# Matmuls of one weight group in series by width in place of alternation, in a two-layer decoder trunk

## Chip, cores and metric

One Trainium2 chip, one core. The metric is the device time of one execution in microseconds; the median of three runs is taken.

## What is computed

Two pre-norm residual layers on 256 tokens of width 2048, in float32. Each layer has three groups of attention heads over one shared normalised input, an output projection, and a gated MLP of inner width 5632 with a causal convolution over three tokens. Cut to its frame:

```python
for l in range(DEPTH):
    h = _rmsnorm(x, attn_norm[l])
    z = jnp.einsum('bsd,de->bse', h, w_in[l])
    ...
    mix = jnp.concatenate([o_a, o_b, o_c], axis=-1)
    x = x + jnp.einsum('bsm,md->bsd', mix, w_o[l])
    h = _rmsnorm(x, ffn_norm[l])
    x = x + _conv_gated_mlp(h, ffn_w_up[l], ffn_conv_w[l], ffn_conv_b[l], ffn_w_down[l])
return _rmsnorm(x, final_norm)
```

## The kernel before

All activations lie transposed, features on the 128 partitions and the 256 tokens along the free axis. All weights lie in HBM as one stream of 128x128 blocks in the order of their use. `load` brings 16 blocks at a time into a `raw` tile (three buffers). `convert` takes a group of 8 blocks (`SUB`) and splits each weight into a rounded part `hi` (line 134, a cast on ScalarE, ACT in the profile) and the rest `lo` (line 135, a subtraction on VectorE, DVE); `hi` and `lo` have four buffers each. An activation tile is split in the same way: it holds 512 columns, the high parts of the 256 tokens and then their low parts. The product to full accuracy is then weight `hi` times all 512 columns, plus weight `lo` times the first 256; the halves of the 512 result columns are added at the end (`total`, lines 227 and 229, or the additions into `x`, lines 726 and 727).

`mm_t` (lines 175 to 189) does this for one output tile of 128 features. It takes a PSUM bank (three under the name `mm`), goes over the k blocks of the inner width and issues two matmuls for each: the 512-column one with `hi` (line 184) and the 256-column one with `lo` (line 185), in alternation. The last block of a chain has them the other way round (lines 187 and 188), so that the chain ends on the 512-column one. `weights`, called for each block, starts the conversion two groups ahead, and the load of later chunks, at the first block of a group. `hooks` lets a chain form the column of the norm (`inv_rms`, line 324) after half of its blocks.

Chains of `mm_t` are: the input projections (k = 16), the output projection in two passes (k = 10 and k = 6, 16 chains each), the up projection of the MLP (k = 16, 88 chains a layer in two halves of 44) and the down projection (k = 22, 16 chains for each half). The stream is counted in groups of 8 from its start. In layer 0 the blocks after the narrow projections begin in the middle of a group, so an up chain there covers 4, 8 and 4 blocks of three groups; in the MLP of layer 1 it covers two whole groups.

Three other helpers use the same stream and are not touched. `mm_t2` does two output tiles at once at the start of a layer. `mm_v` (lines 208 to 223) makes tiles with tokens on the partitions: the activation is stationary, the weights `hi` and `lo` are the moving operand, three matmuls of 512 or 256 columns for each step (lines 218 to 220). `narrow` issues three matmuls of 256 columns for each block (lines 678 to 680). The Tile framework puts the instructions of each engine in order by priority and dependence, so small steps of other work stand between the chains on TensorE (PE), such as attention (lines 386 to 419).

Of the kernel before, what the change touches and what calls it, by code (L numbers as in the profile page):

```python
# [17 lines left out]
T = 256  # L18
# [10 lines left out]
SUB = 8  # L29
# [29 lines left out]
def kernel(ctx: ExitStack, tc: tile.TileContext, xin, pos, wstream, cst, par, fin, out):  # L59
    nc = tc.nc  # L60
# [14 lines left out]
    def slot(dtype=F32):  # L75
        return slots.tile([P, 2 * T], dtype, tag="slot", name=nm("slot"))
# [10 lines left out]
    def bank(tag, bufs):  # L87
        return psum.tile([P, 512], F32, tag=tag, name=nm(tag), bufs=bufs)
# [8 lines left out]
    bounds = [(i, min(SUB, nblk - i)) for i in range(0, nblk, SUB)]  # L97
    sub_of = {b: s for s, (at, n) in enumerate(bounds) for b in range(at, at + n)}

    def load(c):  # L100
        if c >= nch or c in raws:
            return
        n = min(CH, nblk - c * CH)
        t = wpool.tile([P, CH * P], F32, tag="raw", name=nm("raw"), bufs=3)
        nc.sync.dma_start(
            t[:, : n * P], wflat[c * CH * P * P : (c * CH + n) * P * P].rearrange("(p e) -> p e", p=P)
        )
        raws[c] = t
# [12 lines left out]
    def convert(s, between=None):  # L121
        if s >= len(bounds) or s in subs:
            return
        at, n = bounds[s]
        c = at // CH
        load(c)
        o = (at - c * CH) * P
        src = raws[c][:, o : o + n * P]
        hi = wpool.tile([P, SUB * P], F32R, tag="hi", name=nm("hi"), bufs=4)
        lo = wpool.tile([P, SUB * P], F32R, tag="lo", name=nm("lo"), bufs=4)  # L130
        step = SUB // 2 * P if c < 3 else SUB * P
        for o in range(0, n * P, step):
            a = slice(o, min(o + step, n * P))
            nc.scalar.copy(hi[:, a], src[:, a])  # L134
            nc.vector.tensor_tensor(lo[:, a], src[:, a], f(hi[:, a]), ALU.subtract)  # L135
            if between is not None:
                between()
        subs[s] = (hi, lo)

    def weights(b, n=1):  # L140
        s = sub_of[b]
        at = bounds[s][0]
        if b == at:
            convert(s)
            convert(s + 1)
            convert(s + 2)
            load(b // CH + 1)
            load(b // CH + 2)
        o = (b - at) * P
        hi, lo = subs[s]  # L150
        return hi[:, o : o + n * P], lo[:, o : o + n * P]

    cb = [0]
# [21 lines left out]
    def mm_t(moving, hooks={}, tag="mm", bufs=3):  # L175
        ps = bank(tag, bufs)
        k = len(moving)
        for i, mv in enumerate(moving):
            if i in hooks:
                hooks[i]()  # L180
            hi, lo = weights(cb[0])
            cb[0] += 1
            if i < k - 1:
                nc.tensor.matmul(ps, hi, mv, start=(i == 0), stop=False)  # L184
                nc.tensor.matmul(ps[:, :T], lo, mv[:, :T], start=False, stop=False)  # L185
            else:
                nc.tensor.matmul(ps[:, :T], lo, mv[:, :T], start=(i == 0), stop=False)  # L187
                nc.tensor.matmul(ps, hi, mv, start=False, stop=True)  # L188
        return ps

    def mm_t2(moving, hooks={}):
# [287 lines left out]
    for l in range(DEPTH):  # L479
# [4 lines left out]
        if l == 0:  # L484
            first = mm_t2(hx)
            convert(4)
            convert(5)
            squares()
            first.append(mm_t(hx))
            first.append(mm_t(hx, {KT // 2: norm.cols}, "s", 2))  # L490
        else:
            first = mm_t2(hx, {KT // 2: norm.cols})
# [62 lines left out]
        for j in range(2):  # L555
            for h in range(H_FOX):
                if j == 0:
                    fqk.append(slot())
                i = j * H_FOX + h + 1
                u = total(first[i] if i < len(first) else mm_t(hx))  # L560
                nc.gpsimd.tensor_tensor(fqk[h][:, j * T : (j + 1) * T], u, rstd if j else rstd_f, ALU.mult)
                tick()
# [100 lines left out]
        mv = [slot() for _ in range(3)]  # L663
# [52 lines left out]
        for m in range(KT):  # L716
            ps = mm_t([mix[i] for i in order])
# [6 lines left out]
        for m in range(KT):  # L724
            ps = mm_t([mix[i] for i in range(4, 10)])
# [5 lines left out]
        for half in range(2):  # L731
            acts = []
            for i in range(HALF):
                ft = half * HALF + i
                ys = []
                for j in range(2):
                    ps = mm_t(hx, {KT // 2: norm.cols} if rstd is None else {})
# [23 lines left out]
            for m in range(KT):  # L761
                ps = mm_t(acts)
# [136 lines left out]
```

## Time and profile before

| | |
|---|---|
| median of 3 runs | 2298.94 us (2298.13 to 2301.83) |
| span of the profiled execution | 2297.5 us, 1.4 us under the median |
| PE busy | 2270.6 us, 99% |
| VectorE busy | 1580.0 us, 69% |
| ScalarE busy | 1234.2 us, 54% |
| HBM traffic | 178 GB/s over the span |
| granted TensorE clock | 0.997 of full speed |

All times in the profile are of one execution and count from the start of its span. A row of the timeline has a start and a duration. PE's durations are latencies: matmuls overlap in the array, so the distance between the starts of two rows, and not the duration, says how long one holds the engine. Line numbers are those of the kernel before.

### The profile page before, as it was taken

What the parts mean: (1) busy time and instruction counts of PE and PEld (TensorE: products, weight loads), DVE (VectorE), ACT (ScalarE), POOL (GpSimd) and SP (SyncE); (2) the same over time, 40 slices, a digit from 0 to 9 for tenths busy, and PEclk for the clock granted to TensorE, in tenths of its full rate; (3) what the DMA queues carried; (4) which work ended last, traced back from release to release, by engine and by line L of the source; (5) the groups of instructions that cost most, each with busy time, mean ns of one, the idle gap of its engine ahead of it and who ended that gap; (6) DMA issues with size and microseconds to landing.
All of it is one profiled execution on the core that took longest, in us unless ns stands there. A gap on an engine that the chain in (4) does not pass through costs nothing.

```text
span 2297.5 us, 33344 instructions
## 1 busy us (share of the span) xinstructions
PE 2270.6 (99%) x12956; PEld 1965.8 (86%) x12956; DVE 1580.0 (69%) x2512; ACT 1234.2 (54%) x1878; POOL 447.6 (19%) x445
## 2 busy tenths in 40 slices
PE   8999999999999999999999999999999999999997
PEld 7888988888888888888888889888888888888886
DVE  7768768777765577776664777687777556777654
ACT  6456645655543455554454665466555435555543
POOL 5500002222210022221140110032222001222211
PEclk9999999999999999999999999999999999999999
DMA  7544434555555555555555444345555555555553
GB/s 257 186 163 165 149 140 171 183 183 186 188 187 190 184 184 185 185 191 185 189 185 183 152 162 164 129 173 189 188 184 183 186 187 191 188 184 183 185 186 116
DMA packets 60062, 410.59 MB, mean 179 GB/s; under 512 B 6912, under 2 KB 7040, under 8 KB 11136
## 3 DMA queue, kind: packets, MB, share of 16 engines
q1 hardware_dynamic: 59184, 407.40, 49.8%
q8 instruction: 101, 1.65, 0.3%
q10 hardware_dynamic: 720, 1.07, 0.1%
q14 instruction: 57, 0.47, 0.1%
HBM read 406.35 MB, written 2.10 MB: 178 GB/s over the span
## 4 chain that ended last, share of the span: by engine, by line
PE 96%; DVE 3%; issue 1%; ACT 0%; DMA 0%; POOL 0%; DVEq 0%; ACTq 0%
PE mm L184 52%; PE mm L185 26%; PE mm L188 3%; PE mm L218 2%; PE mm L219 2%; PE mm L220 2%; PE s L386 2%; PE mm L187 2%; DVE h L360 1%; PE mm L205 1%; DVE lo L135 1%; PE mm L678 1%; PE mm L679 1%; PE mm L680 1%; PE pv L418 1%
## 5 line engine op out<-in xcount | busy, mean ns | idle before, releaser
L135 DVE TENSOR_TENSOR lo<-raw,hi 128x1024 fp32r<-128x1024 f32 (+1 forms) x775 | 988.7, 1276 | 454.3 <-ACT hi L134 449.7
L184 PE MATMUL mm<-h,hi 128*128 128x512 f32 x3435 | 1225.4, 399 | 0.6 <-DVE x L727 0.6
L134 ACT CAST hi<-raw 128x1024 fp32r<-128x1024 f32 (+1 forms) x775 | 807.4, 1042 | 596.7 <-PE mm L184 444.8
L185 PE MATMUL mm<-h,lo 128*128 128x256 f32 x3435 | 964.1, 281 | 0.0
L184 PEld LDWEIGHTS mm<-h,hi 128*128 128x128 f32 x3435 | 645.5, 188 | 151.6 <-issue 1.7
L185 PEld LDWEIGHTS mm<-h,lo 128*128 128x128 f32 x3435 | 648.5, 189 | 9.8
L184 PE MATMUL mm<-slot,hi 128*128 128x512 f32 x1792 | 640.0, 399 | 3.4 <-DVE x L727 3.4
L185 PE MATMUL mm<-slot,lo 128*128 128x256 f32 x1792 | 503.1, 281 | 0.0
L184 PEld LDWEIGHTS mm<-slot,hi 128*128 128x128 f32 x1792 | 336.7, 188 | 87.0 <-issue 5.1
L185 PEld LDWEIGHTS mm<-slot,lo 128*128 128x128 f32 x1792 | 338.4, 189 | 4.7
L741 POOL TENSOR_TENSOR tmp<-tmp,rstd 128x256 f32<-128x256 f32 x176 | 131.1, 745 | 736.3 <-DVE tmp L229 721.2
L227 ACT COPY tmp<-mm 128x256 f32<-128x256 f32 (+1 forms) x233 | 86.7, 372 | 161.1 <-PE mm L188 159.5
L749 POOL TENSOR_TENSOR tmp<-tmp,tmp 128x256 f32<-128x256 f32 x88 | 120.2, 1366 | 268.6 <-ACT tmp L748 264.9
L355 POOL TENSOR_TENSOR tmp<-tmp,tmp 128x256 f32<-128x256 f32 x64 | 78.5, 1227 | 454.1 <-ACT tmp L350 453.3
L744 ACT ACTIVATE tmp<-tmp,par 128x256 f32<-128x256 f32 x176 | 105.7, 601 | 66.5 <-POOL tmp L741 66.4
L229 DVE TENSOR_TENSOR tmp<-mm,tmp 128x256 f32<-128x256 f32 (+1 forms) x233 | 97.6, 419 | 53.2 <-ACT tmp L227 53.1
L424 DVE TENSOR_TENSOR slot<-tmp,slot 128x256 fp32r<-128x256 f32 x96 | 41.2, 429 | 92.5 <-ACT slot L423 92.5
L423 ACT CAST slot<-tmp 128x256 fp32r<-128x256 f32 x96 | 39.0, 406 | 108.0 <-POOL tmp L749 106.3
L188 PE MATMUL mm<-h,hi 128*128 128x512 f32 x229 | 91.4, 399 | 0.0
L746 DVE SCALAR_TENSOR_TENSOR tmp<-tmp,par,tmp 128x254 f32<-128x254 f32 x176 | 85.0, 483 | 6.2
L745 DVE SCALAR_TENSOR_TENSOR tmp<-tmp,par,tmp 128x255 f32<-128x255 f32 x176 | 83.3, 473 | 1.3 <-ACT tmp L744 1.3
L218 PE MATMUL mm<-hi,h 128*128 128x512 f32 (+1 forms) x192 | 68.3, 356 | 0.0
(183 smaller groups left out, 1815.0 us busy)
## 6 DMA issues: line engine op xcount, KB each, us to landing
raw<-in_w SPq DMA_DIRECT2D x381, 1024.0 KB, 4.8
raw<-in_w SPq DMA_DIRECT2D x12, 256.0 KB, 5.4
x<-in_x SPq DMA_DIRECT2D x8, 256.0 KB, 5.3
out<-x SPq DMA_DIRECT2D x4, 256.0 KB, 2.3
out<-x ACTq DMA_DIRECT2D x4, 256.0 KB, 2.4
raw<-in_w SPq DMA_DIRECT2D x1, 512.0 KB, 3.4
par<-in_par SPq DMA_DIRECT2D x1, 325.0 KB, 6.3
par<-in_par SPq DMA_DIRECT2D x1, 304.0 KB, 5.2
```

What stands on the lines that cost most here:

```text
L134: nc.scalar.copy(hi[:, a], src[:, a])
L135: nc.vector.tensor_tensor(lo[:, a], src[:, a], f(hi[:, a]), ALU.subtract)
L184: nc.tensor.matmul(ps, hi, mv, start=(i == 0), stop=False)
L185: nc.tensor.matmul(ps[:, :T], lo, mv[:, :T], start=False, stop=False)
L188: nc.tensor.matmul(ps, hi, mv, start=False, stop=True)
L218: nc.tensor.matmul(ps[t][:, :n], s_hi, hi, start=(i == 0), stop=False)
L227: nc.scalar.copy(t[:rows], ps[:rows, T : 2 * T])
L229: nc.vector.tensor_tensor(u[:rows], ps[:rows, :T], t[:rows], ALU.add)
L741: nc.gpsimd.tensor_tensor(uu, u, rstd, ALU.mult)
L744: nc.scalar.activation(y, uu, AF.Identity, scale=q_[:, w + 2 : w + 3], bias=q_[:, w + 3 : w + 4])
L746: nc.vector.scalar_tensor_tensor(y[:, 2:], uu[:, : T - 2], q_[:, w : w + 1], y[:, 2:], ALU.mult, ALU.add)
L749: nc.gpsimd.tensor_tensor(ys[0], ys[0], ys[1], ALU.mult)
```

## The change

`mm_t` cuts its blocks into runs that lie in one group of 8. For each run it asks for all weights first, and then issues all 512-column matmuls of the run as one series and all 256-column ones as another. In the first run of a chain the wide series leads (the first matmul has to write all 512 columns of the bank), in the last the narrow one leads (the chain ends wide), and in runs between the wide one leads. In a chain of one run the last wide matmul stands behind the narrow series. The hooks of a run are called ahead of the whole run.

```diff
--- before.py
+++ after.py
@@ -175,17 +175,27 @@
     def mm_t(moving, hooks={}, tag="mm", bufs=3):
         ps = bank(tag, bufs)
         k = len(moving)
-        for i, mv in enumerate(moving):
-            if i in hooks:
-                hooks[i]()
-            hi, lo = weights(cb[0])
-            cb[0] += 1
-            if i < k - 1:
-                nc.tensor.matmul(ps, hi, mv, start=(i == 0), stop=False)
-                nc.tensor.matmul(ps[:, :T], lo, mv[:, :T], start=False, stop=False)
-            else:
-                nc.tensor.matmul(ps[:, :T], lo, mv[:, :T], start=(i == 0), stop=False)
-                nc.tensor.matmul(ps, hi, mv, start=False, stop=True)
+        runs, i = [], 0
+        while i < k:
+            n = min(k - i, SUB - (cb[0] + i - bounds[sub_of[cb[0] + i]][0]))
+            runs.append(range(i, i + n))
+            i += n
+        for r, run in enumerate(runs):
+            for i in run:
+                if i in hooks:
+                    hooks[i]()
+            ws = [weights(cb[0] + i) for i in run]
+
+            def high(part):
+                for i in part:
+                    nc.tensor.matmul(ps, ws[i - run[0]][0], moving[i], start=(i == 0), stop=(i == k - 1))
+
+            n = len(run) if r < len(runs) - 1 else len(run) - 1 if r == 0 else 0
+            high(run[:n])
+            for i in run:
+                nc.tensor.matmul(ps[:, :T], ws[i - run[0]][1], moving[i][:, :T], start=False, stop=False)
+            high(run[n:])
+        cb[0] += k
         return ps
 
     def mm_t2(moving, hooks={}):
```

In the changed file the wide matmuls have line 191 and the narrow ones line 196; other lines behind `mm_t` are 10 higher.

What the order of PE has at the border of two up chains of layer 0 (banks `mm_9249` and `mm_9307`; `h` are the activation tiles, `hi_9225` and `lo_9226` one weight group), before:

```order
L184 MATMUL mm_9249<-h_3722,hi_9225 128x512
L185 MATMUL mm_9249<-h_3722,lo_9226 128x256
L187 MATMUL mm_9249<-h_3723,lo_9226 128x256
L188 MATMUL mm_9249<-h_3723,hi_9225 128x512
L184 MATMUL mm_9307<-h_3708,hi_9225 128x512
L185 MATMUL mm_9307<-h_3708,lo_9226 128x256
L184 MATMUL mm_9307<-h_3709,hi_9225 128x512
L185 MATMUL mm_9307<-h_3709,lo_9226 128x256
```

And the same place now:

```order
L196 MATMUL mm_9249<-h_3722,lo_9226 128x256
L196 MATMUL mm_9249<-h_3723,lo_9226 128x256
L191 MATMUL mm_9249<-h_3720,hi_9225 128x512
L191 MATMUL mm_9249<-h_3721,hi_9225 128x512
L191 MATMUL mm_9249<-h_3722,hi_9225 128x512
L191 MATMUL mm_9249<-h_3723,hi_9225 128x512
L191 MATMUL mm_9307<-h_3708,hi_9225 128x512
L191 MATMUL mm_9307<-h_3709,hi_9225 128x512
L191 MATMUL mm_9307<-h_3710,hi_9225 128x512
L191 MATMUL mm_9307<-h_3711,hi_9225 128x512
L196 MATMUL mm_9307<-h_3708,lo_9226 128x256
L196 MATMUL mm_9307<-h_3709,lo_9226 128x256
```

The four blocks that end one chain and the four that begin the next are in the same group; their wide matmuls now form one series of eight, with narrow series of four on either side of it (the one ahead is the end of a longer one).

The place of the norm column in the first up chain of layer 0 (line 324 before, 334 now; `tmp_3743` is the sum of squares), before:

```order
L185 MATMUL mm_4103<-h_3718,lo_4055 128x256
L184 MATMUL mm_4103<-h_3719,hi_4054 128x512
L185 MATMUL mm_4103<-h_3719,lo_4055 128x256
L324 MATMUL misc_4124<-cs,tmp_3743 128x1 x2
L184 MATMUL mm_4103<-h_3720,hi_4082 128x512
L185 MATMUL mm_4103<-h_3720,lo_4083 128x256
```

And now:

```order
L196 MATMUL mm_4103<-h_3717,lo_4055 128x256
L196 MATMUL mm_4103<-h_3718,lo_4055 128x256
L334 MATMUL misc_4112<-cs,tmp_3743 128x1 x2
L196 MATMUL mm_4103<-h_3719,lo_4055 128x256
L196 MATMUL mm_4103<-h_3720,lo_4083 128x256
L196 MATMUL mm_4103<-h_3721,lo_4083 128x256
```

The column's matmuls stand at nearly the same place in PE's order, now between two narrow matmuls of the middle run.

## Rows read from the trace of the kernel before

**Rows 1.** The page: busy us of the engines, and the chain that ended last.

```profile
PE 2270.6 (99%) x12956; PEld 1965.8 (86%) x12956; DVE 1580.0 (69%) x2512; ACT 1234.2 (54%) x1878; POOL 447.6 (19%) x445
...
PE 96%; DVE 3%; issue 1%; ACT 0%; DMA 0%; POOL 0%; DVEq 0%; ACTq 0%
```

**Rows 2.** Waits: engine and line, for whom, us in total, times, longest.

```profile
ACT hi L134 <- PE mm L184: 444.8, 350, 3.6
...
PE mm L202 <- DVE h L360: 7.1, 1, 7.1
...
PE s L185 <- DVE lo L135: 0.3, 1, 0.3
```

**Rows 3.** Groups of PE by shape: count | busy us, mean ns | idle before.

```profile
L184 PE MATMUL mm<-h,hi 128*128 128x512 f32 x3435 | 1225.4, 399 | 0.6 <-DVE x L727 0.6
...
L184 PE MATMUL mm<-slot,hi 128*128 128x512 f32 x1792 | 640.0, 399 | 3.4 <-DVE x L727 3.4
...
L188 PE MATMUL mm<-h,hi 128*128 128x512 f32 x229 | 91.4, 399 | 0.0
...
L188 PE MATMUL mm<-slot,hi 128*128 128x512 f32 x128 | 51.3, 400 | 0.1
```

**Rows 4.** Busy time by stretch: one up projection, one `mm_v`, one `narrow`.

```profile
core 0: us, PE busy (x) PEld busy (x) DVE busy (x) ACT busy (x) POOL busy (x), PEclk, DMA share, GB/s
775.59:1018.68 243.09, 243.09 (x1378) 210.80 (x1376) 173.27 (x235) 141.85 (x211) 60.28 (x62) 1.00 0.53 186
88.53:109.61 21.08, 21.08 (x94) 17.46 (x93) 10.42 (x9) 8.76 (x10) 0.87 (x2) 1.00 0.56 199
277.98:287.81 9.83, 9.83 (x84) 9.83 (x83) 8.71 (x21) 6.57 (x11) 0.00 (x0) 1.00 0.42 142
```

**Rows 5.** PE's timeline, up projection: start us, duration us; from first to last, three pairs.

```profile
800.20 0.28 PE L185 MATMUL mm<-h,lo 128*128 128x256 f32 x1
...
801.02 0.40 PE L184 MATMUL mm<-h,hi 128*128 128x512 f32 x1
801.26 0.28 PE L185 MATMUL mm<-h,lo 128*128 128x256 f32 x1
```

**Rows 6.** PE's timeline, first and last row of twelve pairs of a down projection.

```profile
667.48 0.28 PE L185 MATMUL mm<-slot,lo 128*128 128x256 f32 x1
...
671.64 0.28 PE L185 MATMUL mm<-slot,lo 128*128 128x256 f32 x1
```

**Rows 7.** PE's timeline, from `mm_t` into the series of 512 of `mm_v`.

```profile
87.84 0.40 PE L188 MATMUL mm<-h,hi 128*128 128x512 f32 x1
88.07 0.40 PE L218 MATMUL mm<-hi,h 128*128 128x512 f32 x1
88.31 0.39 PE L219 MATMUL mm<-lo,h 128*128 128x512 f32 x1
```

**Rows 8.** PE's timeline, from 512 to 256 inside `mm_v`: first and seventeenth of 256.

```profile
109.84 0.28 PE L218 MATMUL mm<-hi,h 128*128 128x256 f32 x1
...
111.75 0.28 PE L219 MATMUL mm<-lo,h 128*128 128x256 f32 x1
```

**Rows 9.** PE's timeline, `mm_v` after an attention block: the ends of six steps.

```profile
182.87 0.39 PE L219 MATMUL mm<-lo,h 128*128 128x512 f32 x1
...
184.25 0.39 PE L219 MATMUL mm<-lo,h 128*128 128x512 f32 x1
```

**Rows 10.** DVE's timeline, the low part of one group.

```profile
800.77 1.23 DVE L135 TENSOR_TENSOR lo<-raw,hi 128x1024 fp32r<-128x1024 f32 x1 [1.16 <-ACT hi L134]
```

**Rows 11.** PE's timeline, the norm column in layer 0's first up chain.

```profile
405.32 0.61 PE L324 MATMUL misc<-cs,tmp 128*128 128x1 f32 x4 [1.39 <-DVE tmp L355]
```

**Rows 12.** PE's timeline, end of a chain of `mm_t` and start of the next.

```profile
775.11 0.28 PE L185 MATMUL mm<-slot,lo 128*128 128x256 f32 x1
...
775.35 0.40 PE L188 MATMUL mm<-slot,hi 128*128 128x512 f32 x1
...
775.82 0.28 PE L185 MATMUL mm<-h,lo 128*128 128x256 f32 x1
```

## The prediction

> **What bounds the kernel now.** I read the page's busy table first, then the chain that ended last, the waits of TensorE, the groups by shape, and then the timeline and the table by stretches to see what one matmul costs beside its neighbours. TensorE is busy for 2270.6 of 2297.5 us and 96% of the chain is PE [rows 1]. Its waits for other engines are few: the largest is 7.1 us once at the start, and one for a converted `lo` tile, 0.3 us [rows 2]. So the time is the sum of the distances from one matmul's start to the next one's, and a change of order on PE is worth what it does to these distances.
>
> The pairs that the change touches are 3435 + 1792 from lines 184 and 185, 229 + 128 from the ends of their chains [rows 3], and 16 of the one chain in another bank, `s`: 5600 in all. The 399 ns that the groups name for a wide matmul is a latency, and latencies overlap. What counts is the spacing. A long stretch of the up projection gives it: 243.09 us for 43 chains of 16 pairs, so 243.09 / 688 = 353.3 ns a pair, at clock 1.00 (the upper level, 2.4 GHz) and with PE busy throughout [rows 4]. Seen singly, three pairs take 1.06 us, from 800.20 to 801.26, and the last 512-column matmul of them holds the engine for 0.24 us [rows 5].
>
> The same trace has series of one width, in the value and narrow projections, each matmul with a weight load of its own as in the pairs. In `mm_v` 93 steps of 512 columns take 21.08 us, 226.7 ns each; in `narrow` 82 steps of 256 columns take 9.83 us, 119.9 ns each, and the counts of weight loads go with those of matmuls [rows 4]. One of each is 346.6 ns, 6.7 ns less than a pair in alternation. That alternation can also run at that pace is seen at 667.48 to 671.64 us: 12 pairs in 4.16 us, 346.7 ns [rows 6]. The extra 6.7 ns is thus not in the columns; it belongs to how the two widths fall on each other in most chains.
>
> **The change, part by part.** *What it removes.* In the written order of the changed program a 512-column matmul follows a 256-column one 571 times among these pairs, against 5240 before; the rest stand in series, mostly of 8 and 16 with some of 4 where a chain begins in the middle of a group. Of the 5600 pairs 4224 are in the MLP (176 up chains of 16, 64 down chains of 22), nearly all at 353.3: 4224 x 6.7 = 28.3 us. The other 1376 (input and output projections) lie between the two paces, so between 0 and 9.2 us; I take 6, two thirds, as both paces occur there. Together 34 us, if every matmul went at the pace of a series.
>
> *What it adds.* Each border between series has a price. From 256 to 512 it is in the trace once at full length: after a chain's last 256s, the 512s at 87.84, 88.07 and 88.31, and then 226.7 each [rows 4]. The first two take 0.47 us against 0.453, 17 ns too much, and the 0.01 us of the rows allows 10 ns either way [rows 7]. From 512 to 256 the first sixteen take 1.91 us (109.84 to 111.75) against 1.92, so nothing, or a few ns gained [rows 8]. A round trip costs some 13 ns (17 less a few), and 571 of them 7.5 us. From both sides: nothing where series fall together as the alternation at 346.7 does; and 20 ns where a series needs as long to settle as it does after an attention block, six steps in 1.38 us (182.87 to 184.25) against 1.36 [rows 9], which makes 11.4 us. I take 7.5, because rows 7 is the same border, from 256 in `mm_t` to 512.
>
> *What it moves.* No instruction is added on any engine and every chain still ends on a 512-column matmul, so the copies out of the bank begin where they did. Weights are asked for at the same place, the first block of a group. In a group that begins with the low series `lo` is needed one matmul earlier, 0.24 us; a `hi` tile in a leading series comes free about 1 us (8 x 0.12) earlier, a `lo` tile in a leading series up to 1.8 (8 x 0.227), and neither later. What covers this is the lead of the conversions: ACT waits 444.8 us in 350 waits for PE to free a `hi` buffer and PE waited 0.3 us for `lo` in all [rows 2], so conversions are ahead by nearly the whole buffer depth. If the cover were gone, the price would be a DVE conversion of 1.23 us [rows 10] per group, far above the gain; I cost it at nothing. DVE and ACT keep their work, 173 and 142 of 243 us in an up stretch [rows 4], so 1.5% less time there does not make either the bound. The hook that forms the norm column is written four pairs earlier in the first up chain of layer 0, yet its matmuls stay at the same place of PE's order, after seven of the eight narrow matmuls of the middle run; PE waits 1.39 us there now [rows 11] and reaches it a little sooner, at most 0.1 us more wait. The 32 short chains of the second output pass in both layers also wait on additions into x; if these set the pace there, 192 x 6.7 = 1.3 us of the gain is not had, which I take off by 0.5.
>
> *Sum.* 34 - 7.5 - 0.5 = 26 us off the profiled span of 2297.5, so 2271.5. The median of the runs, 2298.94, lies 1.4 us above that span, for what is around it; the same above the new one gives 2272.9, say 2273 us.
>
> A rule speaks against any gain, and is a rival below. The Trainium skill, "TensorE: Matmul & The Clock Gate", section "Back-to-back issue gap", gives the warm spacing as the matmul's own columns over 2.4 GHz plus about 2.5 ns. By it a pair is an estimated 325 ns in whatever order, and the sum would be no change. The trace does not agree: 353.3 and 346.7 ns for the same two widths.
>
> **The rivals.** *Series settle as slowly as after attention.* Then 571 x 20 = 11.4 us are given back in place of 7.5: gain 22, 2277 us. This is inside my range. In the other direction, borders that cost nothing give 34 us, 2265.
>
> *A series of 512 in `mm_t` does not settle (slower).* What the trace has of `mm_t` itself is only two 512s in a row at the ends of chains, and these take 0.47 us for two (775.35 to 775.82), 235 each; the two 256s ahead of them take 0.24, 120 each [rows 12]. At these rates a pair in series costs 355 ns, 1.7 more than now, and 5600 pairs cost 9.5 us: 2308. It decides from 233.3 ns per 512 (353.3 less 120): above, the change loses. For it: these are the very operands (moving `h`, stationary `hi`), while `mm_v` swaps their roles and uses one stationary operand twice. Against it: the two 512s of rows 7 start the same way with 0.23 and 0.24 and the third is at pace, and the weights are loaded for each matmul in both.
>
> *Width alone counts.* The cost of a pair would lie in something other than the order, say in the chains' operands, and it stays at 353: 2299, no change. The 346.7 in rows 6, with the operands of the down projection in alternation, speaks against it, and for it that I cannot say why a chain falls into one pace or the other.
>
> That the change does not do what it says is closed by the order: the series are there.
>
> **How the numbers follow.** About 0.2% (4.6 us) is what a measurement of this kernel can tell from no change. My forecast, with slow or free borders in it, has 0.82: 2263 to 2284, the lower end being the whole 34 us with 2 us of error in the rest, the upper one slow borders and 7 us for waits that I cost at nothing. Width alone 0.07, a series that does not settle 0.08, and 0.03 for waits of the conversions that eat half of the gain, which is still faster or just within 0.2%. So faster 0.85, same 0.07, slower 0.08, and the range leaves out the last three cases.
>
> **What would show it.** In the changed profile an up stretch of layer 1, 43 chains, should take about 43 x (16 x 346.7 + 13) = 239.1 us in place of 243.09, and in layer 0, where chains begin in the middle of a group and have two round trips, 239.6. Within a chain the timeline should show 512s at 0.23, 0.24 and then 226 to 227 ns over the rest, and 256s at 120. PE's waits for `lo` and `hi` should stay under 1 us. It is wrong if 512s in series stay near 235, if a pair is still 353, or if new waits for lines 134 and 135 appear in front of a series.

## The result and the profile after

| | before | after |
|---|---|---|
| median | 2298.53 us, 4 runs (2296.55 to 2301.83) | 2278.24 us, 4 runs (2277.20 to 2278.74) |
| ratio, 95% interval | | 0.9909 [0.9895, 0.9923] |
| span of the profiled execution | 2297.5 us | 2275.4 us |

The changed kernel is 20.3 us faster by the medians and 22.1 us by the spans. The forecast was 26 us less, 2273 us in a range of 2263 to 2284. So the direction and the range hold, and the gain came out 4 us smaller than forecast by the spans and over 5 by the medians. (The profiled execution is the fastest of the four, so the new median lies 2.8 us above the new span and not 1.4 as before.)

The page of the changed kernel, busy us of the engines and the chain that ended last by engine:

```profile
PE 2247.6 (99%) x12956; PEld 1970.5 (87%) x12956; DVE 1574.5 (69%) x2512; ACT 1221.3 (54%) x1878; POOL 424.6 (19%) x445
...
PE 96%; DVE 2%; issue 1%; ACT 1%; DMA 0%; SPq 0%; DVEq 0%; ACTq 0%
```

It has the shape of [rows 1]: PE bounds the kernel at 99%, with 23.0 us less of it. The waits of TensorE, and the largest wait of the conversions for it, in the columns of [rows 2]:

```profile
PE mm L212 <- DVE h L370: 6.6, 1, 6.6
PE misc L334 <- DVE tmp L365: 5.2, 3, 2.0
PE mm L191 <- DVE x L737: 3.9, 8, 1.1
...
PE mm L196 <- ACT slot L433: 0.8, 2, 0.4
PE mm L213 <- DVE lo L135: 0.3, 1, 0.3
...
ACT hi L134 <- PE mm L191: 352.1, 286, 4.0
```

The waits are nearly the old ones; only that for `slot`, 0.8 us, is new. None for line 134 or 135 stands in front of a series, and ACT still waits hundreds of microseconds for PE to free `hi` buffers, so the conversions kept their lead. One wait has grown, that for the norm column (line 334, 324 before): it was 3.4 us in two waits. More of it below. The groups by shape, to be read against [rows 3]:

```profile
L191 PE MATMUL mm<-h,hi 128*128 128x512 f32 x3664 | 908.7, 393 | 0.0
L196 PE MATMUL mm<-h,lo 128*128 128x256 f32 x3664 | 493.9, 282 | 0.0
L191 PE MATMUL mm<-slot,hi 128*128 128x512 f32 x1920 | 486.2, 393 | 3.9 <-DVE x L737 3.9
```

The mean latency of a wide matmul fell from 399 to 393 ns. That is about the gain of a pair, but the spacing is what decides. From here on a *border* is a place where the width changes, and a *round trip* is one change from narrow to wide and one back. Two up halves of 44 chains by stretch, from the first matmul's start to the last one's, in the columns of [rows 4]. The first is in layer 0 (chains over 4, 8 and 4 blocks), the second in layer 1 (chains over two whole groups):

```profile
766.67:1012.25 245.58, 245.58 (x1409) 216.13 (x1408) 173.84 (x241) 144.27 (x216) 61.35 (x64) 1.00 0.53 189
1892.98:2137.69 244.71, 244.71 (x1409) 216.30 (x1407) 175.91 (x239) 140.57 (x216) 47.40 (x64) 1.00 0.53 189
```

The 704 pairs of such a stretch at the series' pace, 226.67 + 120.00 = 346.67 ns by the unrounded starts, less the last wide matmul, which the window leaves out, are 243.83 us. Layer 1 is 0.88 us above that, or **20 ns for each of 44 chains**, which have one round trip each. Layer 0 is 1.75 us above it, 20 ns for each of 88 round trips. Before, the two stretches took 248.5 us each from first start to last start; this is where the time came from. How a series runs is seen on the timeline of PE (start us, duration us). Layer 0 first, and then layer 1, where series of 16 meet across chains:

```profile
572.59 2.00 PE L191 MATMUL mm<-h,hi 128*128 128x512 f32 x8
574.43 1.60 PE L196 MATMUL mm<-h,lo 128*128 128x256 f32 x12
575.86 0.86 PE L191 MATMUL mm<-h,hi 128*128 128x512 f32 x3
```
```profile
1930.11 3.82 PE L191 MATMUL mm<-h,hi 128*128 128x512 f32 x16
1933.76 2.08 PE L196 MATMUL mm<-h,lo 128*128 128x256 f32 x16
1935.67 3.82 PE L191 MATMUL mm<-h,hi 128*128 128x512 f32 x16
```

From start to start eight wide ones take 1.84 us, and 8 x 226.7 is 1.81; sixteen take 3.65 against 3.63. Both have about 0.02 to 0.03 us too much whatever their length, so it is lost at the start of the series. The narrow ones take 1.43 for 12 (1.44 at pace) and 1.91 for 16 (1.92), and give back up to 10 ns at theirs. By the unrounded starts the wide distances after a settled narrow series are 233, 236, 228, 233, 231 and then 227 ns, and the narrow ones begin with 113, 119, 120. Together that is 27 ns too much in the wide series and 8 too little in the narrow one, the 20 ns again.

### The profile page after: what moved, and what is told of

The parts are those of the page before. It is cut to its first block, busy times and chain, and to the rows that moved or that the text cites. A ratio compares the mean times of both kernels' runs of the same rounds, so it can differ in the third digit from the quotient of the medians.

```text
span 2275.4 us, 33362 instructions
## 1 busy us (share of the span) xinstructions
PE 2247.6 (99%) x12956; PEld 1970.5 (87%) x12956; DVE 1574.5 (69%) x2512; ACT 1221.3 (54%) x1878; POOL 424.6 (19%) x445
## 3 DMA queue, kind: packets, MB, share of 16 engines
q10 hardware_dynamic: 720, 1.07, 0.1%
## 4 chain that ended last, share of the span: by engine, by line
PE 96%; DVE 2%; issue 1%; ACT 1%; DMA 0%; SPq 0%; DVEq 0%; ACTq 0%
PE mm L191 55%; PE mm L196 28%; PE mm L228 2%; PE mm L229 2%; PE mm L230 2%; PE s L396 2%; DVE h L370 1%; PE mm L688 1%; PE mm L690 1%; PE mm L689 1%; PE pv L428 1%; DVE lo L135 1%; PE misc L349 0%; PE mm L215 0%; PE misc L334 0%
## 5 line engine op out<-in xcount | busy, mean ns | idle before, releaser
L191 PE MATMUL mm<-h,hi 128*128 128x512 f32 x3664 | 908.7, 393 | 0.0
L191 PEld LDWEIGHTS mm<-h,hi 128*128 128x128 f32 x3664 | 665.6, 189 | 125.4 <-issue 1.7
L196 PEld LDWEIGHTS mm<-h,lo 128*128 128x128 f32 x3664 | 484.9, 191 | 27.3 <-DVE lo L135 0.2
L196 PE MATMUL mm<-h,lo 128*128 128x256 f32 x3664 | 493.9, 282 | 0.0
L191 PE MATMUL mm<-slot,hi 128*128 128x512 f32 x1920 | 486.2, 393 | 3.9 <-DVE x L737 3.9
L196 PEld LDWEIGHTS mm<-slot,lo 128*128 128x128 f32 x1920 | 260.0, 190 | 19.2 <-ACT slot L433 1.5
L196 PE MATMUL mm<-slot,lo 128*128 128x256 f32 x1920 | 265.7, 282 | 0.8 <-ACT slot L433 0.8
L365 POOL TENSOR_TENSOR tmp<-tmp,tmp 128x256 f32<-128x256 f32 x64 | 78.8, 1231 | 453.1 <-ACT tmp L360 452.3
L759 POOL TENSOR_TENSOR tmp<-tmp,tmp 128x256 f32<-128x256 f32 x88 | 93.7, 1064 | 303.6 <-ACT tmp L758 300.4
L758 ACT ACTIVATE tmp<-tmp 128x256 f32<-128x256 f32 x88 | 36.8, 418 | 75.4 <-DVE tmp L756 75.4
```

What stands on the lines that cost most here:

```text
L191: nc.tensor.matmul(ps, ws[i - run[0]][0], moving[i], start=(i == 0), stop=(i == k - 1))
L196: nc.tensor.matmul(ps[:, :T], ws[i - run[0]][1], moving[i][:, :T], start=False, stop=False)
L759: nc.gpsimd.tensor_tensor(ys[0], ys[0], ys[1], ALU.mult)
```

## Experiments

Three readings of the round trip stood first. In A it has a fixed price of 20 ns; in B each series has the same first steps and a short one is cut off among them; in C the state of the engine's pipeline is carried over a border, and a round trip costs what an alternation costs, 6.7 ns or less.

**Series of two.** The runs of the changed kernel are cut at two blocks, so that a chain of 16 has seven borders from narrow to wide.

```diff
-            n = min(k - i, SUB - (cb[0] + i - bounds[sub_of[cb[0] + i]][0]))
+            n = min(k - i, 2, SUB - (cb[0] + i - bounds[sub_of[cb[0] + i]][0]))
```

> Series of at most two blocks: 2441 round trips between the widths in place of 571. Theory A, a fixed price of 20 ns for each round trip, wherever it falls (what the 571 of the change cost by its profile, 12.4 us over the pace of a series): 48.8 us, more than the 34 us that the series themselves are worth, so some 15 us slower than the kernel before, 2313 us. Theory B, a series always runs through the same first steps (512s: 233, 236, 228, 233, 231 ns, then 227; 256s: 113, 119, then 120) and a short one is cut off in the middle of them: two 512s 16 ns too much, two 256s 8 ns too little, in sum 22 us, 12 us faster than before, 2286 us. Theory C, the state of the engine is carried over a border and nothing starts anew, so that a border costs what it costs in alternation, 6.7 ns a round trip: 16 us, 2281 us.

Measured: 2279.48 us (2276.35 to 2280.85, 4 runs), ratio 0.9919 [0.9904, 0.9934]. The up half of layer 0 from first start to last:

```profile
768.54:1014.39 245.85, 245.85 (x1409) 214.80 (x1407) 171.24 (x241) 143.15 (x216) 60.51 (x64) 1.00 0.54 189
```

It is 2.02 us above 243.83, for 308 round trips: 6.6 ns each. A fixed 20 ns would have made 6.2 us of it. A falls, and series of two are within the intervals as good as those of eight.

**Series of four**, the same edit with a 4, three round trips a chain.

> Series of at most four blocks, 1105 round trips. A (fixed 20 ns): 22 us of the 34 us are given back, 2286.5 us. B (the same first steps each time): 18.9 us given back, 15 us faster than before, 2283 us. C (6.7 ns a round trip): 7.4 us given back, 2272 us.

Measured: 2284.57 us (2284.33 to 2285.36), ratio 0.9944 [0.9929, 0.9959], and for the same stretch:

```profile
771.42:1017.59 246.17, 246.17 (x1409) 215.89 (x1408) 172.02 (x241) 143.06 (x216) 62.39 (x64) 1.00 0.53 188
```

That is 2.34 us over 132 round trips, 17.7 ns each. Over all of `mm_t` the distances under 300 ns lie 19.2 us above 226.7 and 120.0 ns, close to what B gives (18.9). Length four is the worst: it pays nearly the whole price of settling, three times a chain. So B's sum holds from four blocks on, and C's price for two.

**Groups aligned to chains.** In the changed kernel up to 7 empty blocks are put into the weight stream of each layer behind the narrow projections, and skipped, so that the chains of layer 0 cover whole groups too.

```diff
+        cb[0] += -cb[0] % SUB
...
+        blocks.append(np.zeros((-sum(b.shape[0] for b in blocks) % SUB, P, P), f32))
```

> The change, with four blocks of zeros put into the weight stream after the narrow projections of each layer and skipped, so that every chain of the output, up and down projections of layer 0 begins at the start of a group or at an even place: 458 round trips in place of 571. If the borders are what the change lost, by A 9.2 us and by B 10.0 us remain of its 12.4, so about 2 us less than the change: 2275 to 2276 us, and the up stretch of 43 chains of layer 0 goes from two round trips a chain to one and takes 43 x 20 ns, 0.9 us, less. If the loss has another cause (waits of the conversions, the first matmul of a group), nothing moves: 2278 us and the same up stretch.

Measured: 2276.54 us (2276.02 to 2276.93), ratio 0.9908 [0.9893, 0.9923]. The up half of layer 0 became as short as that of layer 1:

```profile
769.27:1013.97 244.70, 244.70 (x1408) 216.29 (x1407) 175.99 (x239) 140.54 (x216) 47.19 (x64) 1.00 0.53 189
```

This is 0.88 us less than in the changed kernel, 44 round trips at 20 ns. In the median it can hardly be told from the changed kernel.

**Fewer borders.** On the aligned kernel a run covers two groups and begins with the width that the last one ended with, so that there is one border for 16 blocks. The price is that four buffers of `hi` and `lo` belong to two runs.

```diff
-            n = min(k - i, SUB - (cb[0] + i - bounds[sub_of[cb[0] + i]][0]))
+            n = min(k - i, 2 * SUB - (cb[0] + i) % SUB)
...
+            if lead[0]:
+                todo = highs + lows
+            elif run[0] == 0:
+                todo = highs[:1] + lows + highs[1:]
+            else:
+                todo = lows + highs
```

> Aligned stream, series over two groups, and every run begins with the width with which the last one ended, but for one wide matmul that has to stand first in a chain. Some 190 whole round trips and 207 single wide matmuls inside a narrow series remain. A (20 ns each, singles too): 8 us remain, 26 us faster than before, 2272.5 us. B (a single one costs 6 ns and the narrow series behind it gains 8): 4.5 us remain, 2269 us. Rival: both groups of a series have to be converted at its start, so that the four buffers no longer cover the conversions: PE then waits for lines 134 and 135 in the waits, and the time is above 2278 us.

Measured: 2358.66 us, ratio 1.0264 [1.0247, 1.0281]. An up half took 257.58 us. Its largest waits of TensorE:

```profile
PE mm L205 <- DVE lo L135: 41.0, 71, 0.6
PE mm L203 <- DVE slot L443: 18.0, 4, 4.5
```

The rival was right. A run that holds two groups until its second series, with the next two to be converted by its end, takes up all four buffers, and the wait that the prediction had costed at nothing becomes 41.0 us. Four buffers are thus too few for series of two groups; lengths between one and two were not measured.

**Alternation without the swap.** Is it the series that gains, or only that the slow pace is gone? The kernel before has a swap at each chain's end, which puts narrow beside narrow and wide beside wide (lines 187 and 188). Here it is undone and nothing else: pure alternation. Two theories stood. In S alternation has two paces that keep themselves up, 346.7 and 353.3 ns, and what stands just before decides which one it is; in R alternation is slow by itself.

```diff
-            if i < k - 1:
-                nc.tensor.matmul(ps, hi, mv, start=(i == 0), stop=False)
-                nc.tensor.matmul(ps[:, :T], lo, mv[:, :T], start=False, stop=False)
-            else:
-                nc.tensor.matmul(ps[:, :T], lo, mv[:, :T], start=(i == 0), stop=False)
-                nc.tensor.matmul(ps, hi, mv, start=False, stop=True)
+            nc.tensor.matmul(ps, hi, mv, start=(i == 0), stop=False)
+            nc.tensor.matmul(ps[:, :T], lo, mv[:, :T], start=False, stop=(i == k - 1))
```

> The kernel before without the swap at the end of a chain: wide and narrow in strict alternation from chain to chain, no two of a width in a row. Theory S: alternation has two paces that each sustain themselves, 346.7 and 353.3 ns a pair, and what stood before the first pair decides which; the swap at a chain's end is what throws a fast chain back into the slow pace. Then a stretch without interruption keeps one pace over all its chains: the 704 pairs of an up stretch take 244.1 or 248.7 us and nothing between, and the total lies between 2265 and 2298 us, by which stretches fall into which. Rival R: the slow pace belongs to these operands and the swap has no part in it; all four up stretches stay at 248.7 us and the time at 2298 us. A strict alternation that beats the series in a stretch would show that it is not the series as such that gains.

Measured: 2283.52 us (2279.30 to 2286.41, 4 runs), ratio 0.9947 [0.9929, 0.9965]. An up half:

```profile
771.54:1015.48 243.94, 243.94 (x1409) 213.33 (x1408) 177.53 (x240) 145.85 (x216) 62.61 (x64) 1.00 0.53 190
```

With 0.12 us for the last narrow matmul, 244.06 us for 704 pairs is 346.7 ns each, through 44 chains without a round trip to pay. In this execution, the fastest of the four, the other half of layer 0 and the last down half went at 353.3 from their third chain on; the down half had begun at 346.7 and had a wait of 1.1 us in its second chain. So the alternation that is slow in the kernel before runs at the series' pace here, for hundreds of microseconds, and elsewhere in the same program does not.

What the swap does is seen in the kernel before. Its MLP has fast chains only near the beginnings of its halves, as the one of [rows 6], whose last matmul starts at 674.30 us. The chain behind it is slow:

```profile
674.30 0.40 PE L188 MATMUL mm<-slot,hi 128*128 128x512 f32 x1
...
674.88 0.40 PE L184 MATMUL mm<-slot,hi 128*128 128x512 f32 x1
...
677.00 0.40 PE L184 MATMUL mm<-slot,hi 128*128 128x512 f32 x1
```

Six pairs from 674.88 to 677.00 take 2.12 us, 353 ns each, with no wait between. In four of the eight halves the fast chains came to an end at such a swap, and no later chain of any of the eight was fast again.

**Mixed series.** Aligned, with series of 8 in chains of 16 and of 2 in all others.

```diff
-            n = min(k - i, SUB - (cb[0] + i - bounds[sub_of[cb[0] + i]][0]))
+            n = min(k - i, SUB if k == KT else 2, SUB - (cb[0] + i - bounds[sub_of[cb[0] + i]][0]))
```

> Aligned stream, series of up to eight blocks in the chains of 16 and of at most two in the others (output and down projections). By the two runs before, an up stretch takes 244.9 us with aligned series of eight and a down stretch 122.3 us with series of two against 123.5 with longer ones. If a border's price depends on the series around it and not on their number, the four down stretches give 4.8 us and the output projections about 1: 2270 to 2272 us. With a fixed price per border (theory A, 1062 round trips) it would be 21 us over the pace, 2285 us.

Measured: **2273.33 us** (2272.83 to 2274.42), ratio 0.9899 [0.9884, 0.9915]; once more on another occasion 2272.97 (2269.94 to 2274.26), ratio 0.9891. It is the best of the study, 5 us under the changed kernel by the medians and 2 to 4 by the ratios, whose intervals overlap. What it gained over the aligned kernel lies in the short chains: each down half took 122.23 us from first start to last, in place of 123.29. In the first profile the two up halves with a norm column gave 2.6 us of these 4.2 back, so that it came out 1 to 3 us above what was expected. A down half, from the second profile:

```profile
642.86:765.09 122.23, 122.23 (x705) 106.86 (x703) 67.93 (x80) 47.90 (x48) 1.95 (x2) 1.00 0.54 190
```

**Fewer columns.** Two kernels measure what a series pays for its columns. In the first the wide matmuls, but for the first of a chain, have 500 columns; in the second the narrow ones have 192.

```diff
+                    c = 2 * T if i == 0 else 500
+                    nc.tensor.matmul(ps[:, :c], ws[i - run[0]][0], moving[i][:, :c], start=(i == 0), stop=(i == k - 1))
```

> The change with 500 columns in place of 512 in every wide matmul but a chain's first, so the last 12 columns of a chain's low parts are left out. Long series settle at 226.7 ns for 512 and 120.0 for 256, which is columns at 2.4 GHz plus 13.3 ns each. If this is a constant on top of the columns, a settled wide matmul takes 208.3 + 13.3 = 221.7 ns. If matmuls start on a grid of 13.3 ns (226.7 is 17 and 120.0 is 9 of it), 213.3 or 226.7 ns.

> The change with 192 columns in place of 256 in every narrow matmul, so the product of the weights' low part is left out for 64 tokens. If the pace of a narrow series is its columns plus 13.3 ns, it takes 80 + 13.3 = 93.3 ns a matmul and the whole 5600 x 26.7 ns, 149 us, less: 2129 us. If it is held by the weight load that every matmul brings, it does not fall below the 109 ns at which 128-column matmuls follow each other in this trace: 109 to 120 ns, 0 to 62 us less, 2216 to 2278 us.

One execution each: 2255.83 us with 500 columns and 2301.29 with 192. A chain of each in layer 1, 500 columns first:

```profile
1932.44 2.08 PE L197 MATMUL mm<-h,lo 128*128 128x256 f32 x16
1934.36 3.77 PE L192 MATMUL mm<-h,hi 128*128 128x500 f32 x16
1937.97 2.08 PE L197 MATMUL mm<-h,lo 128*128 128x256 f32 x16
```
```profile
1933.55 1.93 PE L196 MATMUL mm<-h,lo 128*128 128x192 f32 x16
1935.32 3.83 PE L191 MATMUL mm<-h,hi 128*128 128x512 f32 x16
```

Sixteen wide ones, the ninth of them a chain's first with 512 columns, take 3.61 us against 3.65. By the unrounded starts the eight behind the narrow series go 221 and 226 ns by turns; those behind the ninth settle at 226.7, as 512 columns do. So neither theory's single figure holds everywhere, and what 500 columns cost depends on what stood before them too. Sixteen of 192 columns take 1.77 us, 111 ns each: a quarter fewer columns bring 9 ns of 120, so it is not the columns alone that hold them then. The second kernel lost elsewhere, above all in layer 0: PE waited 24.8 us for `lo`, 17.9 of them in the MLP of layer 0, and 10.2 us for a `slot` there. A chain with less of PE's time in it needs conversions sooner, which is the danger that the prediction named for the change itself.

**The beginning decides.** If S is right, alternation can be led into the fast pace on purpose. The mixed kernel gets alternation back in the MLP, unswapped, behind one chain in series. In the first kernel the chain after that begins hi lo lo hi hi lo hi lo, in the second with plain alternation. `orders` gives each chain's order as a word.

```diff
+        if c == 0:
+            return "".join("h" * n + "l" * n for n in [SUB] * (k // SUB) + [k % SUB])
+        if c == 1:
+            return PRIMER + "hl" * (k - len(PRIMER) // 2)
+        return "hl" * k
...
-                ps = mm_t(acts)
+                ps = mm_t(acts, order=orders(HALF, m))
```

`PRIMER` is "hllhhlhl" in the first and empty in the second.

> Leaves out nothing. Up and down chains of the MLP in alternation again, no chain's end swapped, behind one chain in series and one that begins hi lo lo hi hi lo hi lo; all else as in e/f_mixed. Theory S (alternation has self-sustaining paces, 346 to 347 and 353.3 ns a pair, and what stood just before decides): this beginning, after a settled narrow series, leads into the fast pace, and 42 up chains hold it: an up half of 44 chains in 243.6 to 244.4 us, against 244.9 in series and 248.8 in the kernel before; about 2268 to 2270 us in all, 3 to 5 under the mixed one. Theory R (alternation is slow by itself, and the fast stretches were chance of a run): 353.3 a pair, some 28 us more than in series, 2296.

> Leaves out nothing. As the primed one, but the second chain begins in plain alternation, so only the three moved matmuls at the start of 8 stretches of the MLP are different. Theory S: a settled narrow series followed by plain alternation falls into the slow pace, 353.3 ns a pair, 248 to 249 us for an up half, and the kernel is 20 to 28 us slower than the primed one, 2290 to 2297; if it is fast as well, the beginning does not matter, and the kernel before is slow only through its swapped chain ends. Theory R: the same as the primed one within 2 us.

> Leaves out nothing. The kernel of the mixed series again, on the chip of the other two, for comparison: 2273 within 2 us by either theory.

Measured on one chip: primed 2281.47 us (2279.77 to 2281.66), ratio 0.9926 [0.9914, 0.9939]; unprimed 2300.83 (2297.25 to 2302.10), ratio 1.0012 [1.0003, 1.0021]; mixed 2272.97. The second up half of layer 0, primed and then unprimed:

```profile
767.70:1011.73 244.03, 244.03 (x1410) 215.10 (x1408) 176.56 (x238) 140.82 (x216) 62.56 (x64) 1.00 0.53 190
642.08:767.59 125.51, 124.42 (x706) 107.75 (x705) 68.68 (x81) 47.94 (x49) 2.05 (x2) 1.00 0.52 185
```
```profile
775.07:1023.65 248.58, 248.58 (x1409) 215.71 (x1408) 176.67 (x238) 140.41 (x216) 62.57 (x64) 1.00 0.53 187
```

The beginnings differ by three moved matmuls in one chain of 44, and the halves by 4.55 us; all four up halves fell so, and the two kernels differ by 19.4 us. (The two first halves differ by 6.0 us; there the unprimed kernel alone also had 3.4 us at half the clock.) The timeline of PE behind the primed beginning, and that of the unprimed kernel behind its own:

```profile
773.31 0.40 PE L192 MATMUL mm<-h,hi 128*128 128x512 f32 x1
773.54 0.40 PE L194 MATMUL mm<-h,lo 128*128 128x256 f32 x2
773.78 0.63 PE L192 MATMUL mm<-h,hi 128*128 128x512 f32 x2
774.26 0.28 PE L194 MATMUL mm<-h,lo 128*128 128x256 f32 x1
774.37 0.40 PE L192 MATMUL mm<-h,hi 128*128 128x512 f32 x1
...
775.76 0.39 PE L192 MATMUL mm<-h,hi 128*128 128x512 f32 x1
```
```profile
781.74 0.40 PE L192 MATMUL mm<-h,hi 128*128 128x512 f32 x1
...
783.86 0.40 PE L192 MATMUL mm<-h,hi 128*128 128x512 f32 x1
```

Four pairs from 774.37 to 775.76 take 1.39 us, 347 ns each; six from 781.74 to 783.86 take 2.12, 353 each. S is shown for the up chains. It failed for the down chains: all four halves went at 353.3 in the primed kernel as well (the second row above, 125.51 us against the mixed kernel's 122.23). There PE waits 1.1 us for the last activation inside the first chain, and its last series has six blocks, so perhaps the beginning does not meet the state that it was made for. That is not shown; other beginnings were not tried.

**Up chains primed, down chains mixed**, each part as it was best:

```diff
-                ps = mm_t(acts, order=orders(HALF, m))
+                ps = mm_t(acts)
```

> Leaves out nothing. Up chains as in the primed kernel (alternation behind one settled series and the beginning hi lo lo hi hi lo hi lo), down chains and all else as in the mixed one. Theory S: the four up halves take 247.4, 244.1, 247.4 and 244.1 us as in the primed kernel, the down halves 122.2 to 122.5 as in the mixed one; the up halves are 0.8 to 2.4 us shorter each than in the mixed kernel, 4 to 6 us together: 2267 to 2269. Theory R: what the down chains do to conversions and banks sets the pace of the up chains too, and they fall back to 353.3 in one half or more, 4.5 us each: 2272 or above.

Measured: 2272.99 us (2272.86 to 2274.71), ratio 0.9893 [0.9876, 0.9909], the same as the mixed kernel. The stretches of layer 0, the up half and the down half before it:

```profile
766.00:1009.98 243.98, 243.98 (x1409) 215.10 (x1407) 176.63 (x238) 140.74 (x216) 62.50 (x64) 1.00 0.53 190
642.03:765.78 123.75, 122.54 (x706) 106.81 (x704) 68.48 (x81) 47.97 (x49) 2.19 (x2) 1.00 0.53 187
```

The up half took what S said, 0.7 us less than the mixed kernel's, but each down half took 1.5 us more than there, of which 1.21 us is a new idle of PE. So the 2267 to 2269 us expected were missed. The largest new wait, and the activation that it waited for on ACT's timeline:

```profile
PE mm L215 <- ACT slot L452: 4.8, 4, 1.2
```
```profile
647.58 1.05 ACT L134 CAST hi<-raw 128x1024 fp32r<-128x1024 f32 x1 [1.07 <-PE mm L210]
648.54 0.41 ACT L778 ACTIVATE tmp<-tmp 128x256 f32<-128x256 f32 x1
650.51 0.40 ACT L452 CAST slot<-tmp 128x256 fp32r<-128x256 f32 x1 [1.56 <-POOL tmp L779]
```

The last activation of the up projection stands behind a conversion on ACT and reaches its slot at 650.9, when the first down chain has been waiting for it. In the mixed kernel the same instructions stand in the same order, but there the conversion began at 645.66, after 0.25 us of waiting for PE in place of 1.07, and the cast at 648.61. So the gain of the up chains went into a wait at the next stage's door; why PE frees this buffer later behind alternation was not looked into further.

## Why the prediction was right, and where it was off

*What bounds.* PE did, at 99%, and the change of order was worth what it did to the distances between matmuls. Nothing moved to another engine.

*What is removed.* The term of 34 us was right. Over all 11057 distances under 300 ns inside `mm_t`, the kernel before lies 34.1 us above 226.7 and 120.0 ns; 27.8 of them lie in the MLP (forecast 28.3) and 6.3 in the projections (forecast 6).

*What is added.* This is the step that failed: "a round trip costs some 13 ns (17 less a few), and 571 of them 7.5 us". It costs 20 ns, and the changed kernel lies 12.4 us above the two paces, of which 571 x 0.020 = 11.4 are round trips. The choice of [rows 7] over [rows 9] was wrong. In [rows 7] the wide matmuls come after just two narrow ones, at a chain's end, and settle by the third; after a settled narrow series they need five. [rows 9], which the prediction put at the end of its range, had the size, and by the unrounded starts nearly the steps too: 224, 231, 236, 228, 233, 231 and then 226 to 227 ns. The rival *series settle as slowly as after attention*, a gain of 22 us and 2277, is what came: 22.1 by spans.

*The account.* Inside `mm_t` 34.1 - 12.4 = 21.7 us. Longer gaps in `mm_t` gave 1.4, and the rest of PE's course took 1.5 more, where the wait for the norm column grew by 1.8: 21.6 of the 22.1. Most of the half microsecond left lies before the first matmul (6.61 us in place of 7.05). The 1.4 us between median and span did not hold, as said above; by the medians the forecast is off for this reason too.

*What is moved.* The conversions kept their lead, as said. The kernel with fewer borders shows what this cover is worth: 82 us against the aligned kernel, 41.0 of them in the wait for `lo`. The 0.5 us for the short output chains was not needed to explain anything, since PE's wait for the additions into `x` stayed as it was (3.9 us against 4.0). The norm column is the second miss. "At most 0.1 us more wait" was for layer 0, where the wait grew from 1.39 to 1.70 us. In layer 1, which had no such wait before, it is 1.54 us now, and something followed that the prediction did not have (last section). Together with the final norm's 2.0 us, which stayed, that makes 5.2 us in place of 3.4.

*The rivals.* A series of 512 does settle in `mm_t`, so the slower side is out; the decisive 233.3 ns is reached only in its first two steps. *Width alone* is out too, as 346.7 is now the pace everywhere. But the doubt noted with it, "that I cannot say why a chain falls into one pace or the other", was the better half of the matter. What the kernel before suffers from is no price of alternation: it is a slow pace into which its swapped chain ends throw it back. Pure alternation and series have the same floor, 346.7 ns, and series of eight and more reached it in every stretch that was read.

*The rule weighed.* The Trainium skill, "TensorE: Matmul & The Clock Gate", section "Back-to-back issue gap", gives the formula for a matmul by itself, which the prediction left out, and says that in a stream of weight loads and matmuls the spacing is set by both. The second half is in line with these runs, where 192 columns took 111 ns, though none of them shows that it is the weight load that holds them. The formula does not fit, as the same pair took 346.7 or 353.3 ns by what stood before it.

*What the prediction said would show it.* The 43 up chains of layer 1 were to take 239.1 us and took 239.4 from the first start to that of the 44th chain; layer 0 was to take 239.6 and took 240.2. The narrow ones go at 120 and the settled wide ones at 226.7, as written; "0.23, 0.24 and then 226 to 227" is the 13 ns again.

## What to carry to other kernels

Where a PE-bound kernel mixes two widths, read the distances between starts over hundreds of matmuls before changing anything: one pattern can have two paces, and three pairs show only one of them. A border's price has to be read after a series as long as the planned one, and from the stretch itself (length less count times pace), since ten-nanosecond rows are too coarse for it. When PE gets a few microseconds faster, look at what is handed over at the ends of stages: that is where the gain went in the last experiment.

## What the runs showed of the hardware

**Two paces that last.** The same alternation of 512 and 256 columns with a weight load each, at a granted clock of 1.00, ran at 346.7 ns a pair over 44 chains of one execution and at 353.3 over more than 40 of another, and a start that differs by three moved matmuls led into one or the other. By the unrounded starts the slow one repeats 241, 120, 236, 113, 233, 117 ns and the primed fast one 230, 117. What state inside the engine this is, no run here shows.

**The clock after a short wait.** At the norm column of layer 1 the changed kernel's PE was almost idle for 1.9 us and then ran at the lower clock for a while. The table by stretch and the timeline:

```profile
1523.40:1525.30 1.90, 0.36 (x4) 0.16 (x3) 1.90 (x4) 1.88 (x5) 1.22 (x1) 1.00 0.56 237
1526.40:1529.80 3.40, 3.40 (x9) 2.65 (x8) 0.93 (x4) 0.32 (x2) 0.00 (x0) 0.50 0.44 164
1529.80:1533.20 3.40, 3.40 (x23) 3.05 (x22) 1.65 (x2) 1.78 (x4) 1.50 (x1) 1.00 0.36 149
```
```profile
1525.29 0.61 PE L334 MATMUL misc<-cs,tmp 128*128 128x1 f32 x4 [1.54 <-DVE tmp L365]
1525.76 0.60 PE L196 MATMUL mm<-h,lo 128*128 128x256 f32 x3
1526.19 3.81 PE L191 MATMUL mm<-h,hi 128*128 128x512 f32 x9
1529.84 0.61 PE L349 MATMUL misc<-tmp,cs 128*128 128x128 f32 x4
```

From 1526.40 to 1529.80 the granted clock is 0.50, 1.2 GHz, and nine wide matmuls take 3.65 us where 9 x 0.23 would be 2.07. So 1.6 us more were lost behind the wait of 1.54 us. But such a wait does not settle it: in layer 0 of the same execution, behind 1.70 us, there was no drop; the mixed kernel, with 2.0 us in both layers, had a drop in both in one execution and only in layer 1 in the other; and the primed kernel, with the same 2.0 us, had none. The kernel before had such a stretch elsewhere, from 30.27 to 33.69 us, where the changed one has none, so in sum it hardly bears on the gain. It explains part of why the first up half of layer 1 gained 1.1 us and the second 3.8.
